# Top-k key selection with one candidate word and two small instructions per bit

## The chip, the cores and the metric

The kernel runs on one core of a Trainium2 chip. The metric is device time in microseconds (us) of one launch; lower is better. The engines are named as the profile names them: PE (matrix multiplication; PEld is its weight load), DVE (vector), ACT (scalar), POOL (GpSimd) and SP (its queue issues most DMAs).

## What is computed

The reference is one inference step of a two-layer decoder for a prompt of 1024 tokens and for 8 sequences of 8 new tokens each. Layer 0 mixes with RWKV-7, layer 1 with sparse attention, and each layer has a feed-forward part. The change lies in the sparse attention. There, an indexer gives every query a score for every key, and only the 256 keys with the highest scores are attended to:

```python
def select_keys(qi, wi, ki, pos_q, topk):
    L = ki.shape[1]
    logits = jnp.einsum('bthd,bsd->bths', qi.astype(F32), ki.astype(F32)) * IDX_DIM ** -0.5
    score = jnp.einsum('bths,bth->bts', jax.nn.relu(logits), wi.astype(F32))
    pos_k = jnp.arange(L)
    adm = pos_k[None, None, :] <= pos_q[None, :, None]
    _, idx = lax.top_k(jnp.where(adm, score, -jnp.inf), topk)
    valid = idx <= pos_q[None, :, None]
    return idx, valid
```

Ties go to the key with the lower index. The attention that follows is a softmax over the chosen keys.

## The kernel before

The 1024 prompt tokens are worked on in two groups. Group A (`GA`) is the 64 sample tokens and the first 512 prompt tokens, group B (`GB`) the last 512. Activations lie with features on the 128 partitions and tokens along the free axis. Every large product is three matmuls, high times high, low times high and high times low part (line 140, tiles `hi`/`lo` or `uh`/`ul` against `wh`/`wl`), into PSUM tiles `o` of 512 columns, of which there are four. DVE empties those of a residual product into `xr` (line 388). For group B one such matmul has 512 columns, for group A 320 or 256.

Layer 1's attention of a group goes by tiles of 128 queries. `att_post` normalises the projections and makes the indexer's scores in a tile `sc` (matmuls `ip`, DVE line 1149). `topk` turns scores into a bias of 0 or -1e30 in place. `att_tile` then makes attention scores (matmuls `sp`, lines 1168 and 1169; DVE line 1264 adds the bias), the softmax (ACT line 1268), transposes (`pt`) and sums over values (`po`). Queries before position 256 need no selection. Four calls of `topk` are left:

- group A, prompt tiles 3 and 4 together: scores of 384 and 512 keys for 128 queries each, beside the attention of tiles 1 and 2 and the sample's indexer (`sample_index`, matmuls `kip`, `il`, `iw`);
- the sample: 64 queries by 2056 keys, beside the attention of tiles 3 and 4; its bias goes through HBM into `att_sample2`, which starts with the transposes `qzp`;
- group B, tiles 0 and 1: 640 and 768 keys, beside `att_post` of tiles 2 and 3;
- group B, tiles 2 and 3: 896 and 1024 keys, beside the attention of tiles 0 and 1.

`topk` finds the 256th largest score of each query by its bits. Scores are taken as 32-bit words; `xm` is all ones for a query with fewer than 256 scores at or above zero, so that negative words can be searched by the same steps. From bit 30 down to bit 0, five things are done: a candidate word `cand` is the found word `m` with this bit set; `cf` is `cand` with the signs turned by `xm`; `count` counts the scores at or above `cf` read as a float, one instruction for each of the two score tiles (one for the sample), with the sum in `cnt`; `ok` says whether that is 256 or more; `m` takes `cand` where `ok` holds. For the upper 15 bits the counts read `ups`, 16-bit copies of the high halves of the scores, and for the lower 16 bits the scores themselves. Then equal scores are ranked (`teq`, `trk`) and the bias is written.

These routines are generators. `together` takes one step of each in turn, so a `topk` bit stands beside a step of an attention tile. A further generator, `side`, carries independent work: the rest of layer 0 and the projections of group B beside group A's attention, and layer 1's output projection and feed-forward of group A beside group B's attention. In group A's attention `RATES` gives it no steps inside `together` and it is written behind; in group B's it gets 0.2 or 0.3 of a step each round. A scheduler then sets the order of instructions on each engine when the program is built, and each engine works its own list in order. So what stands on PE between two attention products is settled before the run.

## Time and profile before

| | |
|---|---|
| median of 3 runs | 4378.32 us (4348.06 to 4389.85) |
| the profiled execution | 4376.47 us |
| its span, first to last instruction | 4374.7 us |
| mean granted TensorE clock | 0.912 |
| PE busy | 4008.7 us (92%) |
| DVE busy | 2647.1 us (61%) |
| ACT busy | 1681.9 us (38%) |
| POOL busy | 971.5 us (22%) |

A busy share is a mean over stages with different limits. Idle time of an engine costs something only in the stage where that engine's work ends last. A granted clock of 1.00 is 2.4 GHz; the other level is half of it, and a mean between the two tells how much of a stretch was at either.

### The profile page before, as it was taken

How to read it: one execution, taken by the hardware profiler on the slowest of the kernel's cores; microseconds unless marked ns; L12 is line 12 of the kernel's file. 1: busy time of each engine (PE TensorE's matmuls, PEld its weight loads, DVE VectorE, ACT ScalarE, POOL GpSimd, SP SyncE). 2: the span in 40 equal slices, each digit the busy share in tenths (PEclk: the TensorE clock that was granted, in tenths of full speed). 3: DMA queues.
4: the chain of work that ended last, by engine and by line, in shares of the span. 5: the costliest groups of instructions: out<-in, count | busy, mean ns of one | idle time of the engine just before them, and what ended most of it. 6: DMA issues, size and time to landing. Idle time of an engine off the chain costs nothing. (4 is left out here: it accounts for less than half of the span.)

```text
span 4374.7 us, 77889 instructions
## 1 busy us (share of the span) xinstructions
PE 4008.7 (92%) x31096; PEld 3205.7 (73%) x31096; DVE 2647.1 (61%) x6822; ACT 1681.9 (38%) x3169; POOL 971.5 (22%) x762
## 2 busy tenths in 40 slices
PE   7997899998999999989899888989778999999999
PEld 5796566666777799988655565778667667998887
DVE  5513766565677655552887964442899965555444
ACT  5533544443345333332444333332443333333333
POOL 1321222222333222211111122222110000222222
PEclk7797779998798999998899999998879999999999
DMA  6675222333221122234332145444211111322332
GB/s 224 211 237 183 66 65 78 99 89 95 59 56 51 45 80 82 78 114 140 102 84 67 53 153 193 141 128 151 69 50 41 40 39 34 116 87 90 96 96 87
DMA packets 506749, 433.94 MB, mean 99 GB/s; under 512 B 93777, under 2 KB 451777, under 8 KB 501202
## 3 DMA queue, kind: packets, MB, share of 16 engines
q1 hardware_dynamic: 500498, 391.20, 30.2%
q0 software_dynamic: 5888, 37.75, 2.5%
q8 instruction: 245, 4.01, 0.4%
q14 instruction: 118, 0.97, 0.1%
HBM read 360.48 MB, written 67.87 MB: 98 GB/s over the span
## 5 line engine op out<-in xcount | busy, mean ns | idle before, releaser
L126 POOL TENSOR_TENSOR wl<-w,wh 128x1024 fp32r<-128x1024 f32 (+1 forms) x258 | 615.8, 2391 | 2330.8 <-ACT wh L122 2076.9
L140 PE MATMUL o<-hi,wh 128*128 128x512 f32 (+4 forms) x2592 | 891.8, 347 | 27.3 <-ACT hi L144 23.6
L140 PE MATMUL o<-lo,wh 128*128 128x512 f32 (+4 forms) x2592 | 890.7, 345 | 18.4 <-DVE lo L145 14.1
L140 PE MATMUL o<-hi,wl 128*128 128x512 f32 (+4 forms) x2592 | 886.3, 343 | 2.5 <-DVE wl L126 2.3
L122 ACT CAST wh<-w 128x1024 fp32r<-128x1024 f32 (+3 forms) x388 | 396.4, 1035 | 985.8 <-PE o L140 816.0
L388 DVE SCALAR_TENSOR_TENSOR xr<-o,mods,xr 128x256 f32<-128x256 f32 (+1 forms) x816 | 463.3, 570 | 292.9 <-PE o L140 281.0
L140 PEld LDWEIGHTS o<-hi,wh 128*128 128x128 f32 (+1 forms) x2592 | 499.2, 194 | 86.6 <-ACT hi L144 28.8
L140 PE MATMUL o<-uh,wh 128*128 128x320 f32 (+2 forms) x1536 | 522.1, 340 | 41.5 <-DVE xr L388 33.0
L140 PEld LDWEIGHTS o<-lo,wh 128*128 128x128 f32 (+1 forms) x2592 | 500.2, 193 | 74.2 <-DVE lo L145 20.1
L140 PEld LDWEIGHTS o<-hi,wl 128*128 128x128 f32 (+1 forms) x2592 | 499.1, 193 | 50.8 <-issue 10.0
L140 PE MATMUL o<-uh,wl 128*128 128x320 f32 (+2 forms) x1536 | 515.3, 336 | 1.8 <-POOL wl L126 1.1
L140 PE MATMUL o<-ul,wh 128*128 128x320 f32 (+2 forms) x1536 | 516.7, 336 | 0.0
L140 PEld LDWEIGHTS o<-uh,wh 128*128 128x128 f32 x1536 | 294.3, 192 | 80.3 <-DVE xr L388 41.0
L140 PEld LDWEIGHTS o<-uh,wl 128*128 128x128 f32 x1536 | 294.2, 192 | 29.8 <-issue 5.7
L140 PEld LDWEIGHTS o<-ul,wh 128*128 128x128 f32 x1536 | 294.7, 192 | 28.0 <-issue 5.8
L126 DVE TENSOR_TENSOR wl<-w,wh 128x1024 fp32r<-128x1024 f32 (+2 forms) x130 | 183.6, 1412 | 216.5 <-ACT wh L122 212.1
L145 DVE TENSOR_TENSOR ul<-z,uh 128x512 fp32r<-128x512 f32 (+1 forms) x128 | 128.5, 1004 | 164.2 <-ACT uh L144 164.1
L1018 PE MATMUL o<-wl,hi 128*128 128x256 f32 (+2 forms) x648 | 188.1, 292 | 6.9 <-POOL wl L126 6.9
L1018 PE MATMUL o<-wh,hi 128*128 128x256 f32 (+2 forms) x648 | 187.1, 291 | 6.9 <-ACT hi L144 6.9
L1018 PE MATMUL o<-wh,lo 128*128 128x256 f32 (+2 forms) x648 | 183.9, 291 | 0.0
L1268 ACT ACTIVATE sm<-sm,st 128x128 f32<-128x128 f32 (+7 forms) x128 | 99.3, 776 | 139.4 <-DVE st L1267 83.8
L1018 PEld LDWEIGHTS o<-wl,hi 128*128 128x128 f32 (+1 forms) x648 | 126.8, 196 | 9.1 <-POOL wl L126 9.1
(411 smaller groups left out, 7063.1 us busy)
## 6 DMA issues: line engine op xcount, KB each, us to landing
w<-in_w_up SPq DMA_DIRECT2D x128, 512.0 KB
w<-in_w_down SPq DMA_DIRECT2D x128, 512.0 KB
wa<-in_w_ada SPq DMA_DIRECT2D x96, 512.0 KB
w<-in_rw_w_rkv SPq DMA_DIRECT2D x48, 512.0 KB
w<-in_att_w_in SPq DMA_DIRECT2D x32, 512.0 KB
RA<-pt SPq DMA_DIRECT2D x48, 288.0 KB
RB<-pt SPq DMA_DIRECT2D x48, 256.0 KB
in<-RA SPq DMA_DIRECT2D x32, 320.0 KB
```

The costliest lines, as they stand in the source:

```text
L122: nc.scalar.copy(h[:kp, :n], w[:kp, :n])
L126: eng.tensor_tensor(out=l[:kp, :n], in0=w[:kp, :n], in1=h[:kp, :n], op=ALU.subtract)
L140: nc.tensor.matmul(o[0:M, 0:c1 - c0], a, b[:, c0:c1], start=(i == 0 and q == 0), stop=(i == n - 1 and q == 2))
L145: (lo_eng or self.nc.vector).tensor_tensor(out=lo, in0=src, in1=hi, op=ALU.subtract)
L388: nc.vector.scalar_tensor_tensor(out=xm[:, p0:c1], in0=o[:, p0 - c0:c1 - c0], scalar=self.mods[l][:, j * 8 + m, 8:9], in1=xm[:, p0:c1], op ...
L1018: nc.tensor.matmul(o[0:n, 0:cw], a, w, start=(k == 0 and q == 0), stop=(k == 7 and q == 2))
L1268: nc.scalar.activation(out=sm[:, 0:L], in_=sm[:, 0:L], func=AF.Exp, scale=-1.0, bias=mn[:, 0:1], accum_out=sums)
```

## The change

`topk` keeps one word, `cf`, which is always the next candidate with its sign turned already. After the count, `no` is the current bit where the count was too small and 0 elsewhere. One instruction then makes the next candidate: `cf` xor `no` xor the next lower bit. So `cand`, `m`, `xm`, `ok` and the predicated copy are gone, and a bit has two small instructions beside its counts where it had four. The 16-bit copies are gone as well, with their step of the generator; all 31 counts read the 32-bit scores. The sample's call names one tile fewer in its placement.

```diff
-        m = T1("tm", [128, n], I32)[0:R]
-        cand = T1("tcand", [128, n], I32)[0:R]
         cf = T1("tcf", [128, n], I32)[0:R]
-        xm = T1("txm", [128, n], I32)[0:R]
-        ok = T1("tok", [128, n], I32)[0:R]
+        no = T1("tno", [128, n], I32)[0:R]
         junk = T1("tj", [128, Lm], BF16)[0:R]
 
-        ups = []
-        for i, s in enumerate(scs):
-            u = T1("tu%d" % i, [128, Lm], BF16)[0:R, 0:s.shape[1]]
-            nc.vector.tensor_copy(u, s.bitcast(BF16).rearrange("p (l b) -> p l b", b=2)[:, :, 1])
-            ups.append(u)
-        yield
-
-        def count(th, op, src):
-            for i, s in enumerate(src):
+        def count(th, op):
+            for i, s in enumerate(scs):
...
-        count(0.0, ALU.is_ge, scs)
-        nc.vector.tensor_scalar(out=xm, in0=cnt, scalar1=float(TOPK) - 0.5, scalar2=-1.0, op0=ALU.is_lt, op1=ALU.mult)
-        nc.vector.memset(m, 0)
+        count(0.0, ALU.is_ge)
+
+        nc.vector.tensor_scalar(out=no, in0=cnt, scalar1=float(TOPK) - 0.5, scalar2=-1.0, op0=ALU.is_lt, op1=ALU.mult)
+        nc.vector.tensor_scalar(out=cf, in0=no, scalar1=1 << 30, scalar2=None, op0=ALU.bitwise_xor)
+        th = cf.bitcast(F32)
         yield
         for b in range(30, -1, -1):
-            nc.vector.tensor_scalar(out=cand, in0=m, scalar1=1 << b, scalar2=None, op0=ALU.bitwise_or)
-            nc.vector.tensor_tensor(out=cf, in0=cand, in1=xm, op=ALU.bitwise_xor)
-            count(cf.bitcast(F32), ALU.is_ge, ups if b >= 16 else scs)
-            nc.vector.tensor_scalar(out=ok, in0=cnt, scalar1=float(TOPK) - 0.5, scalar2=None, op0=ALU.is_ge)
-            nc.vector.copy_predicated(m, ok, cand)
-            yield
-        nc.vector.tensor_tensor(out=cf, in0=m, in1=xm, op=ALU.bitwise_xor)
-        th = cf.bitcast(F32)
-        count(th, ALU.is_gt, scs)
+            count(th, ALU.is_ge)
+            nc.vector.tensor_scalar(out=no, in0=cnt, scalar1=float(TOPK) - 0.5, scalar2=float(1 << b), op0=ALU.is_lt, op1=ALU.mult)
+            if b:
+                nc.vector.scalar_tensor_tensor(out=cf, in0=no, scalar=1 << (b - 1), in1=cf, op0=ALU.bitwise_xor, op1=ALU.bitwise_xor)
+            else:
+                nc.vector.tensor_tensor(out=cf, in0=no, in1=cf, op=ALU.bitwise_xor)
+            yield
+        count(th, ALU.is_gt)
```

The built programs are the same on every engine up to the first selection of group A, and the same again on PE from 162 matmuls after the end of group B's attention on. In between the order has moved. In the changed kernel's rows, line 1187 is the count, 1197 makes `no`, 1199 the next `cf`, and the lines behind the search stand nine lower than before.

On DVE, two bits of group B's second selection beside the attention of tiles 0 and 1 (`sc` are the score tiles, `ql` a query's low part, `PT` a transposed probability tile). Before:

```order
L1204 TENSOR_SCALAR tcand<-tm 128x2
L1205 TENSOR_TENSOR tcf<-tcand,txm 128x2
L1197 TENSOR_SCALAR tj,cnt<-sc_35136,tcf 128x896
L1197 TENSOR_SCALAR tj,cnt<-sc_35137,tcf 128x1024
L1163 TENSOR_TENSOR ql<-qt,qh 64x512
L1207 TENSOR_SCALAR tok<-cnt 128x2
L1208 COPY_PREDICATED tm<-tok,tcand 128x2
L1204 TENSOR_SCALAR tcand<-tm 128x2
L1205 TENSOR_TENSOR tcf<-tcand,txm 128x2
```

Now:

```order
L1199 SCALAR_TENSOR_TENSOR tcf<-tno,tcf 128x2
L1187 TENSOR_SCALAR tj,cnt<-sc_34998,tcf 128x896
L1187 TENSOR_SCALAR tj,cnt<-sc_34999,tcf 128x1024
L1197 TENSOR_SCALAR tno<-cnt 128x2
L1199 SCALAR_TENSOR_TENSOR tcf<-tno,tcf 128x2
L1187 TENSOR_SCALAR tj,cnt<-sc_34998,tcf 128x896
L1278 COPY PT<-pt 128x256
L1187 TENSOR_SCALAR tj,cnt<-sc_34999,tcf 128x1024
```

Between two pairs of counts two small instructions stand now instead of four. Over the four selections 13 emptyings of line 388 in group B and 7 in group A have moved behind the selection beside which they stood.

On PE, from the last indexer product of group B (`ip`) to the first attention score of tile 0 (`sp`), which follows the first selection of group B. `uh`, `ul` are the feed-forward's inner activations of group A, side work. Before:

```order
L1168 MATMUL ip<-kS,qh 128x512
L1169 MATMUL ip<-kS,ql 128x512
L140 MATMUL o<-uh,wl 128x320
L140 MATMUL o<-uh,wh 128x256
...
L140 MATMUL o<-ul,wh 128x320
L140 MATMUL o<-uh,wl 128x320
L1168 MATMUL sp<-kS,qh 128x512
L1169 MATMUL sp<-kS,ql 128x512
```

Now:

```order
L1168 MATMUL ip<-kS,qh 128x512
L1169 MATMUL ip<-kS,ql 128x512
L140 MATMUL o<-uh,wh 128x320
L140 MATMUL o<-ul,wh 128x320
...
L140 MATMUL o<-ul,wh 128x256
L140 MATMUL o<-uh,wl 128x256
L1168 MATMUL sp<-kS,qh 128x512
L1168 MATMUL sp<-kS,qh 128x128
```

193 matmuls of line 140 stood between, 72 stand there now, while on DVE, behind the last line 1149, 17 pairs of counts have become 14; at the last score product of group B's attention the side work is 169 such matmuls behind where it was. They come behind that attention, before the output projection of group B.

On PE, from the last value product of group A's prompt tiles (`po`) to the first transposes of the sample's attention (`qzp`), which wait for nothing of the selection but stand in the order behind it. `hi`, `lo` are group B's activations, side work. Before:

```order
L1291 MATMUL po<-PT,V 64x128 x7
L1296 MATMUL po<-c_ident,st 64x128 x2
L140 MATMUL o<-hi,wh 128x512
L140 MATMUL o<-lo,wh 128x512
...
L140 MATMUL o<-hi,wh 128x512
L140 MATMUL o<-lo,wh 128x512
L1462 MATMUL qzp<-c_ident,qns 128x64 x8
```

Now:

```order
L1282 MATMUL po<-PT,V 64x128 x7
L1287 MATMUL po<-c_ident,st 64x128 x2
L140 MATMUL o<-hi,wl 128x512
L140 MATMUL o<-hi,wh 128x512
...
L140 MATMUL o<-uh,wh 128x512
L140 MATMUL o<-ul,wh 128x512
L1453 MATMUL qzp<-c_ident,qns 128x64 x8
```

302 matmuls of line 140 stood between, 261 stand there now. With 19 more that have gone from before the last `po`, the side work is 60 matmuls behind where it was at `qzp`, and has caught up by the end of group B's feed-forward of layer 0.

## Rows read from the trace of the kernel before

**Rows 1.** The page's first part: the span, then by engine the busy us (share of the span) and count of instructions.

```profile
span 4374.7 us, 77889 instructions
...
PE 4008.7 (92%) x31096; PEld 3205.7 (73%) x31096; DVE 2647.1 (61%) x6822; ACT 1681.9 (38%) x3169; POOL 971.5 (22%) x762
```

**Rows 2.** Busy time of each engine in stretches of the span (from and to in us, the length, then busy us of PE, PEld, DVE, ACT and POOL with counts of instructions in brackets; last the granted TensorE clock, the DMA share and GB/s). 2190 to 2321 is group A's first selection, 2368 to 2527 the sample's bits and 2527 to 2555 its ranks, 3100 to 3303 group B's first selection (from 3257 on it is behind the last `ip`), 3303 to 3532 its second. 3532 to 3705 is the attention of group B's tiles 2 and 3. The last two are stretches of feed-forward alone, of group A and of group B.

```profile
2190.00:2321.00 131.00, 122.46 (x574) 70.75 (x572) 116.41 (x422) 58.51 (x150) 22.55 (x18) 0.95 0.32 86
...
2368.00:2527.00 159.00, 135.46 (x679) 94.33 (x677) 149.67 (x312) 50.60 (x94) 19.22 (x9) 0.91 0.18 52
2527.00:2555.00 28.00, 22.04 (x82) 16.90 (x81) 27.39 (x43) 5.59 (x8) 6.20 (x2) 0.88 0.25 76
...
3100.00:3257.00 157.00, 123.99 (x621) 100.02 (x620) 141.38 (x374) 68.31 (x125) 17.85 (x8) 0.78 0.16 51
3257.00:3303.00 46.00, 36.20 (x234) 34.17 (x233) 44.89 (x136) 11.15 (x17) 7.37 (x3) 0.85 0.20 58
3303.00:3512.00 209.00, 187.61 (x1195) 138.98 (x1193) 193.31 (x604) 70.61 (x141) 14.33 (x6) 0.94 0.15 41
3512.00:3532.00 20.00, 11.84 (x40) 7.60 (x40) 19.91 (x57) 5.12 (x9) 0.00 (x0) 0.70 0.00 0
3532.00:3705.00 173.00, 172.94 (x1223) 128.93 (x1222) 93.20 (x286) 69.59 (x123) 11.91 (x5) 0.99 0.15 40
3850.00:3900.00 50.00, 49.35 (x369) 48.84 (x368) 25.05 (x65) 16.54 (x24) 12.09 (x5) 1.00 0.28 85
4050.00:4100.00 50.00, 50.00 (x218) 40.60 (x217) 22.03 (x25) 17.99 (x25) 15.06 (x6) 1.00 0.34 102
```

**Rows 3.** PE's waits from 2190 to 2555: who waited for whom, total us, times, longest.

```profile
PE o L140 <- DVE xr L388: 12.9, 3, 8.6
PE sp L1169 <- DVE tok L1207: 5.3, 3, 2.7
```

**Rows 4.** DVE's groups of instructions from 2180 to 3520, different shapes together: the four small instructions of a bit over all selections, and the 16-bit copies (count | busy us, mean ns | idle before).

```profile
L1207 DVE TENSOR_SCALAR tok<-cnt 128x2 int32<-128x2 f32 (+1 forms) x124 | 32.0, 258 | 1.4
L1204 DVE TENSOR_SCALAR tcand<-tm 128x2 int32<-128x2 int32 (+1 forms) x124 | 22.7, 184 | 2.3
L1205 DVE TENSOR_TENSOR tcf<-tcand,txm 128x2 int32<-128x2 int32 (+1 forms) x124 | 22.1, 178 | 2.5
L1208 DVE COPY_PREDICATED tm<-tok,tcand 128x2 int32<-128x2 int32 x93 | 20.3, 218 | 1.5
...
L1208 DVE COPY_PREDICATED_SCALAR tm<-tok,tcand 64x1 int32 x31 | 6.3, 204 | 0.6
...
L1190 DVE COPY tu<-sc 128x384 bf16<-128x384 bf16 (+5 forms) x6 | 5.2, 886 | 0.0
...
L1190 DVE COPY tu<-ssc 64x2056 bf16<-64x2056 bf16 x1 | 1.2, 1222 | 0.0
```

**Rows 5.** DVE in order of time, one bit of group A's first selection with nothing between (start us, duration us).

```profile
2302.45 0.15 DVE L1204 TENSOR_SCALAR tcand<-tm 128x2 int32<-128x2 int32 x1
2302.64 0.16 DVE L1205 TENSOR_TENSOR tcf<-tcand,txm 128x2 int32<-128x2 int32 x1
...
2304.28 0.17 DVE L1207 TENSOR_SCALAR tok<-cnt 128x2 int32<-128x2 f32 x1
2304.48 0.16 DVE L1208 COPY_PREDICATED tm<-tok,tcand 128x2 int32<-128x2 int32 x1
```

**Rows 6.** DVE in order of time, a small instruction of group B's first selection with other work behind it.

```profile
3158.78 0.15 DVE L1207 TENSOR_SCALAR tok<-cnt 128x2 int32<-128x2 f32 x1
3158.85 0.74 DVE L1149 SCALAR_TENSOR_TENSOR sc<-rl,pr,sc 128x512 f32<-128x512 f32 x1
```

**Rows 7.** DVE and POOL in order of time, one small instruction of the same selection.

```profile
3203.53 2.39 POOL L126 TENSOR_TENSOR wl<-w,wh 128x1024 fp32r<-128x1024 f32 x1 [7.87 <-ACT wh L122]
...
3203.79 2.16 DVE L1207 TENSOR_SCALAR tok<-cnt 128x2 int32<-128x2 f32 x1
```

**Rows 8.** DVE in order of time, an instruction of the form of the new line 1199 on floats, in a normalisation.

```profile
1914.80 0.17 DVE L169 SCALAR_TENSOR_TENSOR rsAb<-rsAa,ms 128x5 f32<-128x5 f32 x1
```

**Rows 9.** DVE's groups by shape, 2180 to 3520: the sample's counts on 32-bit scores (`ssc`) and on their 16-bit copy (`tu`); then, prompt and sample and all shapes together, all counts on copies.

```profile
L1197 DVE TENSOR_SCALAR_CACHE_REDUCE tj<-ssc,tcf 64x2056 bf16<-64x2056 f32 x17 | 39.9, 2344 | 0.5
L1197 DVE TENSOR_SCALAR_CACHE_REDUCE tj<-tu,tcf 64x2056 bf16<-64x2056 bf16 x15 | 35.1, 2342 | 0.3
...
L1197 DVE TENSOR_SCALAR_CACHE_REDUCE tj<-tu,tcf 128x384 bf16<-128x384 bf16 (+3 forms) x105 | 119.8, 1141 | 1.8
```

**Rows 10.** DVE's emptying of residual products by shape, 2180 to 3520 (512 columns: group B's, 256: group A's).

```profile
L388 DVE SCALAR_TENSOR_TENSOR xr<-o,mods,xr 128x512 f32<-128x512 f32 x128 | 94.9, 745 | 55.2 <-PE o L140 54.8
...
L388 DVE SCALAR_TENSOR_TENSOR xr<-o,mods,xr 128x256 f32<-128x256 f32 x85 | 40.8, 481 | 8.3 <-PE o L140 8.0
```

**Rows 11.** PE in order of time, at the sample's selection, where it waited for DVE's emptying.

```profile
2506.75 0.40 PE L140 MATMUL o<-uh,wl 128*128 128x512 f32 x1
2515.73 0.80 PE L140 MATMUL o<-uh,wh 128*128 128x512 f32 x1 [8.58 <-DVE xr L388]
...
2516.75 0.63 PE L140 MATMUL o<-uh,wl 128*128 128x512 f32 x1
2517.18 0.63 PE L140 MATMUL o<-uh,wh 128*128 128x512 f32 x1
```

More of the change, by code (lines that the diff above doesn't have):

```diff
@@ L1405, in att_mixed @@
                 tiles = [None] + [self.att_tile(g, i, p2, S[i], 512) for i in range(1, 5)]
-                smp = [self.sample_index(p3, ssc, gather, ki_rows, csm), self.topk(p3, [ssc], 64, {"tj": ("kis", 1), "tu0": ("rls", 1), "teq": ("kiraw", 2), "trk": ("kiraw", 2)},
+                smp = [self.sample_index(p3, ssc, gather, ki_rows, csm), self.topk(p3, [ssc], 64, {"tj": ("kis", 1), "teq": ("kiraw", 2), "trk": ("kiraw", 2)},
                                                                                                    lambda s: [s[:, a * 1024:a * 1024 + 1024].rearrange("r (b c) -> r c b", b=2)[:, c0:c0 + 256]
```

## The prediction

> **What bounds the kernel now.** I read first the page's busy times [rows 1]. PE is busy 92% of the span and DVE 61%, so the first guess is that work on DVE is free. That share is a mean, however, so next I cut the span at the four selections [rows 2]. There it is the other way round. In group B's first selection DVE is busy 186.3 of 203 us (141.38 and 44.89) and PE 160.2, at a granted clock of 0.78 to 0.85; in its second DVE has 213.2 of 229 us and PE 199.5. In the sample's bits and ranks DVE has 177.1 of 187 us and PE 157.5. Only group A's first selection is nearer to PE: 122.46 of 131 us, against 116.41 for DVE. In the stretch after the selections, from 3532 to 3705, PE has 172.94 of 173 us and DVE 93.2. So the kernel changes its bound: DVE sets the pace beside a selection, PE sets it elsewhere.
>
> PE's waits confirm it [rows 3]: two of those in group A's attention are for the emptying of a product on DVE (12.9 us) and for `tok`, a small instruction of the search (5.3 us). One of them is seen in order of time [rows 11]: PE stands for 8.58 us, and its next matmuls come 0.43 us apart (2516.75 to 2517.18) instead of some 0.23; that is 1.2 GHz instead of 2.4.
>
> PE's idle time is what there is to win: 8.5, 23.5 and 6 us in group A and the sample, 33, 9.8, 21.4 and 8.2 us in group B [rows 2], 110 us in all. PE's work itself is not changed, and the list that PE works through is fixed. So a shorter selection gains only as much as PE then idles less, and what the scheduler has moved out of the selection's time must be paid for behind it.
>
> **The change part by part.** *Two small instructions less per bit.* With nothing between, small instructions start 0.20 us apart [rows 5] (2304.28 to 2304.48), so two less give 0.40 us a bit, 31 bits 12.4 us, four selections 49.6 us. The groups agree: all small instructions together have 32.0 + 22.7 + 22.1 + 20.3 + 6.3 = 103.4 us [rows 4], half of it 51.7. I take 50. The lower bound: where other work follows at once, a small instruction holds DVE for 0.07 us only [rows 6] (3158.78 to 3158.85), which makes 124 x 2 x 0.07 = 17 us. I keep near the upper end because in these stretches the bits mostly follow each other. The new instruction of line 1199 is not in the trace on integers; the same form on floats takes 0.17 us [rows 8], as much as the `tcf` before it, so I count it at that. It could cost no less than `tcf`'s 0.16, and at twice that it would take 124 x 0.17 = 21 us of the 50 away, which the low end of the range covers.
>
> One of these small instructions took 2.16 us [rows 7], while POOL worked for 2.39 us on a split: DVE stood until POOL was done. Such waits are in the 51.7 and nearly not in the 49.6. The Trainium skill (SBUF — State Buffer, "Who interferes with whom") says that VectorE and GpSimd share a port pair by an exclusive lock, and that an instruction with two SBUF inputs or a plain `tensor_scalar` contends for it. By that the two instructions that stay can each take over a wait of the two that go, so the waits would not be halved; the sum by it would be 49.6 instead of 51.7. The trace agrees with the lock as far as the one row goes.
>
> *No 16-bit copies.* Their seven instructions have 5.2 + 1.2 = 6.4 us [rows 4], shared by the number of keys 2.3 us in group A and 4.1 in group B. Nothing replaces them if a count costs the same on either kind of word, and it does: 2344 ns on 32 bits and 2342 on 16 for the sample's 2056 keys [rows 9]. The Trainium skill (VectorE: DVE Perf Modes, "The perf-mode tier table (the rule you actually need)") speaks against the change here: a `tensor_scalar` on bf16 in SBUF runs at 4x and on fp32 at 2x. By this rule alone the copies would halve their counts, and the sum would turn to a loss; the trace disagrees for the form that also writes a sum, by the pair of 2344 and 2342 ns.
>
> *One round less.* `topk` has one step fewer, so two rounds of group B's attention carry 0.2 of a side step less each: 21.3 instead of 21.7 in all, still 21 whole steps. That costs nothing. The few instructions at a selection's head and end (the clearing of `m`, the last xor) are under 0.3 us each time and I leave them out.
>
> *What the order moves out.* In group A's part 7 emptyings of 745 ns [rows 10] leave the selections, 5 us of DVE, and in group B's 13 of 481 ns, 6 us. With them go side matmuls: 60 of 512 columns in group A's part and 169 of 320 or 256 in group B's. They are paid for later at PE's full pace, 50 us / 218 = 0.229 us each and 50 us / 369 = 0.135 us each [rows 2]: 13.7 and 22.9 us. The emptyings cost nothing there, since DVE is half idle in those stretches (93.2 of 173 us, 22.0 of 50).
>
> *The sum.* Group A and the sample: 25 + 2.3 + 5 = 32 us shorter on DVE, 13.7 us paid back, 18 left. But half of that is from the first selection, where PE has only 8.5 of 131 us to give, so I take two thirds, 12 us. Group B: 25 + 4.1 + 6 = 35 us shorter, 22.9 paid back, 12 left; PE idles 72 us there, so this is not capped. Together 24 us. The profiled execution took 4376.47 us, 1.8 us more than its span and 1.9 us less than the median of the runs shown. 4376.5 - 24 = 4352 us is the forecast; the ends of the sum are 0 (with the 17 us for the small instructions: 17 + 6.4 + 11 = 34 saved, 36.6 paid back) and 56 us (all of DVE's relief).
>
> **The rivals.** *All of the relief arrives.* The moved matmuls find places where PE now stands: in the sample's attention behind the selection, or beside group B's tiles. Then nothing is paid back and the time is 4376.5 - 56 = 4320 us. For it speaks PE's idle time of 110 us; against it that PE is full from 3532 on [rows 2], where group B's 169 matmuls go.
>
> *Nothing arrives.* The scheduler has moved as much PE work out as the selections get shorter: 36.6 us. If small instructions are mostly hidden among other work [rows 6], DVE saves 34 us, and the time stays at 4377 us. The place where this is nearest is the join before group B's first attention scores: 121 of the 193 side matmuls are gone there (16 us), while the 17 bits that stood behind the last `ip` in the order have become 14, and a bit is worth 0.40 us.
>
> *Slower: PE starves at the joins.* With 72 matmuls (10 us) between the last `ip` and the first `sp`, and some 14 bits of search beside them, PE stands for most of the time that was 46 us long, falls to 1.2 GHz, and starts the next tile slowly. The stall of [rows 11] shows the price: matmuls 0.43 us apart instead of 0.23, 3.6 us behind each wait if I take it to last for 18 matmuls. If that comes at all four selections (14 us) and DVE's saving is the low 23 us without the emptyings, against 36.6 us paid back, the time is 4376.5 + 14 + 13.6 = 4404 us. It decides when DVE saves less than PE has to make up. PE's idle time of 72 us in group B's selections speaks for it; against it, that the search still has 0.40 us less in every bit.
>
> *Slower: 32-bit counts cost more.* If the 15 counts on copies came to cost twice as much on the scores, their 119.8 us [rows 9] would come on top, 58 us would go, and the time would be near 4440 us. The pair of 2344 and 2342 ns is against it. This is what the tier table of the Trainium skill, named above, would make of the change.
>
> **How the numbers follow.** The forecast of 4352 us has a chance of 0.54, all of the relief 0.18, nothing 0.20, starving 0.07 and dear counts 0.01. The range must leave out no more than 2 in 10: from 4318, just below the full relief, to 4386, which takes in the case of no gain and the half per cent that single runs of this kernel differ by (4348 to 4390). It leaves out 0.08 for the two slow cases and as much again for misjudged sums. About 1%, or 44 us, is what a measurement of this kernel can tell from no change. Faster by more needs less than 4334.5 us: the full relief, and the better tail of the forecast, 0.23. Slower by more needs over 4422 us: the dear counts and a worse case of starving, 0.05. That leaves 0.72 within 1%.
>
> **What the changed profile would show.** The counts keep their durations to a few ns, with twice `no` and `cf` at 0.13 to 0.20 us between them; DVE's busy time falls by 50 to 60 us. A bit of group A's first selection alone takes some 1.85 us instead of 2.25. The sample's bits end about 25 us sooner than at 2527, and group B's second selection about 50 us sooner than at 3532, reckoned from the start. PE's stretch after it is full and some 20 us longer. Up to 2190 us nothing moves. The forecast is wrong if PE's idle time in the selections does not fall (then nothing arrives), if PE's clock there drops under 0.78 (starving), or if the matmuls that moved stand in what are now PE's gaps (full relief). A line 1199 of 0.3 us or more would take a fifth or more of the gain.

## Result and the profile after

The changed kernel takes 4335.24 us (median of 12 runs, 4327.12 to 4357.13), the kernel before 4378.3 us in the runs beside it. The ratio is 0.9909 with a 95% interval of 0.9889 to 0.9929, so some 40 us are gone (31 to 49) where 24 were forecast. Run once more beside three of the experiments, it gave 0.9919 (0.9879 to 0.996).

The page after, its span and busy times:

```profile
span 4346.6 us, 77619 instructions
PE 4005.2 (92%) x31096; PEld 3205.6 (74%) x31096; DVE 2601.4 (60%) x6563; ACT 1679.1 (39%) x3169; POOL 972.6 (22%) x762
```

Against [rows 1] DVE has 45.7 us less to do, and PE's count is the same. The next rows are DVE's groups from 2180 to 3520 (count | busy us, mean ns | idle before), different shapes together: the new small instructions, and the sample's counts, now all on 32-bit words.

```profile
L1197 DVE TENSOR_SCALAR tno<-cnt 128x2 int32<-128x2 f32 (+1 forms) x124 | 29.7, 240 | 1.0
L1199 DVE SCALAR_TENSOR_TENSOR tcf<-tno,tcf 128x2 int32<-128x2 int32 (+1 forms) x120 | 26.5, 221 | 1.7
L1201 DVE TENSOR_TENSOR tcf<-tno,tcf 128x2 int32<-128x2 int32 (+1 forms) x4 | 0.6, 154 | 0.1
...
L1187 DVE TENSOR_SCALAR_CACHE_REDUCE tj<-ssc,tcf 64x2056 bf16<-64x2056 f32 x32 | 74.9, 2340 | 0.5
```

The small instructions have 29.7 + 26.5 + 0.6 = 56.8 us, where [rows 4] had 103.4. A count costs 2340 ns, as much as either kind in [rows 9]. One bit of group A's first selection alone, DVE in order of time (start, duration; READ_ACCUMULATOR is the end of a count):

```profile
2256.37 0.75 DVE L1187 TENSOR_SCALAR_CACHE_REDUCE tj<-sc,tcf 128x512 bf16<-128x512 f32 x1
2257.04 0.08 DVE L1187 DVE_READ_ACCUMULATOR tj<-sc,tcf 128x1 f32 x1
2257.16 0.17 DVE L1197 TENSOR_SCALAR tno<-cnt 128x2 int32<-128x2 f32 x1
2257.36 0.16 DVE L1199 SCALAR_TENSOR_TENSOR tcf<-tno,tcf 128x2 int32<-128x2 int32 x1
2257.56 0.61 DVE L1187 TENSOR_SCALAR_CACHE_REDUCE tj<-sc,tcf 128x384 bf16<-128x384 f32 x1
2258.10 0.08 DVE L1187 DVE_READ_ACCUMULATOR tj<-sc,tcf 128x1 f32 x1
2258.22 0.75 DVE L1187 TENSOR_SCALAR_CACHE_REDUCE tj<-sc,tcf 128x512 bf16<-128x512 f32 x1
```

From one count to the same count of the next bit it is 1.85 us (2256.37 to 2258.22), and the small instructions start 0.20 us apart, as in [rows 5].

To see where the time went, both traces are cut at the same events instead of the same times. The columns are those of [rows 2]. The stretches are, in this order: the sample's upper 15 bits; its lower 16; from its last count to the transposes `qzp`; the upper 15 bits of group B's first selection; the upper 15 and then the lower 16 of its second; and everything from the first count of group A's first selection to the last matmul. Before:

```profile
2369.30:2450.09 80.79, 70.00 (x377) 45.65 (x375) 75.99 (x171) 28.57 (x60) 5.82 (x3) 0.94 0.17 46
2450.09:2527.30 77.21, 64.46 (x294) 47.89 (x295) 72.71 (x143) 21.63 (x34) 13.71 (x7) 0.89 0.20 58
2527.30:2570.77 43.47, 32.76 (x128) 25.40 (x126) 31.93 (x46) 10.40 (x14) 11.91 (x7) 0.92 0.40 114
3127.29:3233.95 106.66, 77.71 (x341) 58.81 (x341) 96.64 (x264) 54.81 (x102) 7.17 (x3) 0.73 0.13 43
3324.15:3410.40 86.25, 77.41 (x488) 57.16 (x485) 79.95 (x249) 25.46 (x55) 4.79 (x2) 0.92 0.12 33
3410.40:3512.00 101.60, 95.94 (x640) 71.04 (x638) 92.94 (x301) 38.15 (x73) 7.14 (x3) 0.98 0.18 46
2191.86:4368.93 2177.07, 1997.27 (x12086) 1576.53 (x12084) 1389.71 (x3301) 782.46 (x1326) 410.44 (x238) 0.94 0.30 90
```

After:

```profile
2377.44:2442.82 65.38, 60.31 (x342) 40.37 (x340) 64.66 (x125) 26.81 (x52) 7.16 (x3) 1.00 0.21 58
2442.82:2512.96 70.14, 59.83 (x284) 45.30 (x283) 68.44 (x109) 20.65 (x33) 14.65 (x6) 0.95 0.21 65
2512.96:2547.04 34.08, 25.50 (x99) 20.14 (x99) 31.54 (x48) 7.60 (x10) 7.72 (x5) 0.85 0.27 71
3107.96:3196.21 88.25, 59.26 (x280) 45.69 (x278) 82.80 (x218) 43.84 (x84) 10.63 (x5) 0.71 0.15 47
3287.56:3367.54 79.98, 76.74 (x505) 57.10 (x504) 74.51 (x217) 28.98 (x60) 7.08 (x3) 0.97 0.18 47
3367.54:3463.77 96.23, 91.46 (x588) 67.64 (x586) 84.46 (x258) 34.98 (x68) 4.74 (x2) 0.93 0.11 30
2205.72:4340.49 2134.77, 1980.63 (x12089) 1568.00 (x12087) 1344.11 (x3044) 781.35 (x1327) 412.30 (x238) 0.95 0.30 92
```

Two things are read from the last rows. From the first count on the kernel takes 2134.77 us instead of 2177.07, 42.3 less. PE's idle time in it (the length less PE's busy time) fell from 179.8 to 154.1 us, which is 25.7 of that. The other 16.6 are PE's busy time: the same matmuls at a granted clock that was more often 2.4 GHz. To three digits the mean clock of these rows is 0.943 before and 0.949 after; what is missing to 1.000 makes 124 and 109 us, a difference of 15.

Ahead of the first count nothing has changed in the order on any engine but two copies of under 2 us, and yet this count began at 2191.86 us before and at 2205.72 after; in the other profiled executions of this study at anything from 2183 to 2212. So single executions scatter by up to 29 us in code that is the same. Behind the first count they do so less: two executions of one kernel agreed there within 1.4 us (changed kernel 2134.8 and 2136.1; the kernel of the first experiment 2143.6 and 2144.7). But the kernel before and two kernels of the experiments that are changed in group B alone (e4 and e10) have the same order on PE, DVE, ACT and POOL up to one emptying behind the sample's last output, and it starts 593.4, 600.0 and 588.4 us behind their first counts (at 2191.86, 2196.88 and 2187.71 us):

```profile
2785.26 0.75 DVE L388 SCALAR_TENSOR_TENSOR xr<-o,mods,xr 128x512 f32<-128x512 f32 x1 [0.63 <-PE o L140]
2796.89 0.75 DVE L388 SCALAR_TENSOR_TENSOR xr<-o,mods,xr 128x512 f32<-128x512 f32 x1 [0.63 <-PE o L140]
2776.12 0.75 DVE L388 SCALAR_TENSOR_TENSOR xr<-o,mods,xr 128x512 f32<-128x512 f32 x1 [0.64 <-PE o L140]
```

I therefore take 12 us as what a comparison of two executions from the first count can tell. Behind group B's first count it is 3 us: kernels with the same order there took 1279.2 and 1282.2 us (before and e3), and 1266.1, 1268.1 and 1268.2 us (the changed kernel twice and e4).

### The profile page after: what moved, and what is told of

Its sections match the earlier page's. It is cut to its first block, busy times and chain, and to the rows that moved or that the text cites. A ratio compares the mean times of both kernels' runs of the same rounds, so it can differ in the third digit from the quotient of the medians.

```text
span 4346.6 us, 77619 instructions
## 1 busy us (share of the span) xinstructions
PE 4005.2 (92%) x31096; PEld 3205.6 (74%) x31096; DVE 2601.4 (60%) x6563; ACT 1679.1 (39%) x3169; POOL 972.6 (22%) x762
## 5 line engine op out<-in xcount | busy, mean ns | idle before, releaser
L140 PE MATMUL o<-hi,wh 128*128 128x512 f32 (+4 forms) x2592 | 886.7, 345 | 27.4 <-ACT hi L144 22.7
L140 PE MATMUL o<-uh,wh 128*128 128x320 f32 (+2 forms) x1536 | 522.1, 340 | 39.4 <-DVE xr L388 29.7
L1187 DVE TENSOR_SCALAR_CACHE_REDUCE tj<-sc,tcf 128x384 bf16<-128x384 f32 (+2 forms) x192 | 180.4, 940 | 2.4
L1259 ACT ACTIVATE sm<-sm,st 128x128 f32<-128x128 f32 (+7 forms) x128 | 99.3, 776 | 154.1 <-DVE st L1258 106.4
```

Of the source, the lines that this page charges most:

```text
L140: nc.tensor.matmul(o[0:M, 0:c1 - c0], a, b[:, c0:c1], start=(i == 0 and q == 0), stop=(i == n - 1 and q == 2))
L1187: nc.vector.tensor_scalar(out=junk[:, 0:L], in0=s, scalar1=th if isinstance(th, float) else th[:, i:i + 1], scalar2=None, op0=op, op1=ALU. ...
L1259: nc.scalar.activation(out=sm[:, 0:L], in_=sm[:, 0:L], func=AF.Exp, scale=-1.0, bias=mn[:, 0:1], accum_out=sums)
```

## Experiments

Theory 1 is the prediction's: a shorter selection is worth DVE's time, less the PE work that the new order leaves to make up. Theory 2 holds the new order for a chance gain. Theory 3, formed after the first results: the scheduler takes counts on 16-bit words for shorter than they are, so it lays too little other work beside the upper bits, and PE stands. Theory 3 has a part that no run shows, what the scheduler takes a count for; its consequences can be tested. The table has for each kernel the ratio over whole runs, and from its profiled execution the times from group A's first count: to the first count of group B (all of group A's attention and what is made up behind it) and to the end, with PE's idle and busy time in the latter.

| kernel | ratio [95%] | to B's first count, us | to the end, us | PE idle | PE busy |
|---|---|---|---|---|---|
| before | 1 | 897.9 | 2177.1 | 179.8 | 1997.3 |
| e1, no copies | 0.9881 [0.9845, 0.9918] | 878.4 | 2143.6 | 169.1 | 1974.5 |
| e1 again | 0.9890 [0.9848, 0.9931] | 879.4 | 2144.7 | 163.4 | 1981.3 |
| e2, two small only | 0.9961 [0.9938, 0.9984] | 881.7 | 2164.3 | 161.5 | 2002.8 |
| e3, new in group A | 0.9904 [0.9871, 0.9938] | 871.3 | 2153.5 | 164.3 | 1989.2 |
| e4, new in group B | 0.9953 [0.9930, 0.9976] | 902.2 | 2170.4 | 173.5 | 1996.9 |
| e5, two unread | 0.9937 [0.9912, 0.9962] | 874.2 | 2146.0 | 160.7 | 1985.3 |
| e6, more side work | 0.9887 [0.9852, 0.9921] | 869.6 | 2140.5 | 159.7 | 1980.8 |
| e7, all 16-bit | 0.9995 [0.9978, 1.0012] | 898.2 | 2183.3 | 185.1 | 1998.3 |
| e8, copies unread | 0.9951 [0.9928, 0.9974] | 881.3 | 2147.2 | 172.6 | 1974.6 |
| e9, more side work twice | 0.9879 [0.9824, 0.9935] | 865.6 | 2137.0 | 155.5 | 1981.5 |
| e10, before with more side work | 1.0010 [0.9980, 1.0040] | 893.2 | 2179.0 | 180.2 | 1998.8 |
| after | 0.9909 [0.9889, 0.9929] | 868.6 | 2134.8 | 154.1 | 1980.6 |
| after again (e11) | 0.9919 [0.9879, 0.9960] | 868.0 | 2136.1 | 153.8 | 1982.3 |

**No copies, four small instructions (e1, and once more).** The kernel before; the copies are left out, and every count reads the scores.

```diff
...
-            u = T1("tu%d" % i, [128, Lm], BF16)[0:R, 0:s.shape[1]]
-            nc.vector.tensor_copy(u, s.bitcast(BF16).rearrange("p (l b) -> p l b", b=2)[:, :, 1])
...
-            count(cf.bitcast(F32), ALU.is_ge, ups if b >= 16 else scs)
+            count(cf.bitcast(F32), ALU.is_ge, scs)
```

> The kernel before with one part of the change alone: the 16-bit copies are gone and all 31 counts read the 32-bit scores; the four small instructions of a bit stay. Theory 1 (DVE's time beside a selection comes back, less the PE work that goes behind it): only the copies' 6.4 us leave DVE, so 2 to 6 us less, ratio 0.999 (0.997 to 1.001). Theory 2 (the order that the scheduler happens to lay decides, not DVE's time): the order moves here too, so the ratio may lie anywhere between 0.992 and 1.008. Counts of equal duration on both kinds of word, 2340 to 2346 ns for the sample, in either theory.

> The kernel before without the 16-bit copies, a second time: the first gave 0.9881 (0.9845 to 0.9918) where 6.4 us were expected. Theory 3: 108 more side matmuls stand before the last value product of group B than in the kernel before (11348 and 11240) and 30 more before the sample's last output (8062 and 8032), 15 and 7 us of PE, with the copies' 6.4 us near 28 us: ratio 0.9935 (0.990 to 0.996). Theory 1: 0.999.

Measured: 0.9881 and 0.989, and 33 and 32 us less from the first count on. Theory 1 falls as to this part: copies of 6.4 us of DVE cannot give 33. The first ratio is also below theory 2's 0.992 and the second below theory 3's 0.990. In whole runs the ratios mean 52 and 48 us of 4378, as much as the whole change or more; why the traces give less is open.

**Two small instructions, copies and 16-bit counts kept (e2).** The changed kernel with the copies put back and the upper 15 counts on them; the diff shows the count.

```diff
-            count(th, ALU.is_ge)
+            count(th, ALU.is_ge, ups if b >= 16 else scs)
```

> The changed kernel with the 16-bit copies put back and the upper 15 counts on them: only the two small instructions per bit are gone. Theory 1: 50 of 56 us of DVE's relief, so about nine tenths of the 40 us of the change, ratio 0.992 (0.990 to 0.995). Theory 2: not tied to that, anywhere between 0.988 and 1.004.

Measured: 0.9961 (17 us, 7 to 27), outside theory 1's 0.990 to 0.995, and 12.8 us less from the first count on: 16.2 less in group A's part and 3 more in group B's. PE's idle time fell by 18.3 us, its busy time rose by 5.5. The upper 15 bits of group B's second selection, and the whole from the first count:

```profile
3308.67:3388.16 79.49, 69.66 (x355) 49.52 (x354) 66.89 (x185) 22.10 (x47) 4.70 (x2) 0.74 0.13 34
2211.81:4376.06 2164.25, 2002.80 (x12086) 1580.20 (x12084) 1348.66 (x3049) 782.99 (x1326) 413.27 (x238) 0.94 0.30 91
```

Its granted clock there is 0.74, where the kernel before has 0.92 and the changed one 0.97: in bits that are shorter, with 355 matmuls beside them instead of 488, PE stands for 10 of 79 us and more of its matmuls run at 1.2 GHz. Behind group B's first count PE's busy time rose by 11 us (1202.2 against 1191.2) while its idle time fell by 7.6. That is the starving of the prediction's third rival, in this stretch of this kernel.

**New routine in one group only (e3 in A, e4 in B).**

```diff
-                self.together(RATES["post2B"], post[2:4], [self.topk(tk, S[0:2])])
+                self.together(RATES["post2B"], post[2:4], [self.topk_old(tk, S[0:2])])
...
-            self.together(RATES["tile0B"], tiles[0:2], [self.topk(tk, S[2:4])])
+            self.together(RATES["tile0B"], tiles[0:2], [self.topk_old(tk, S[2:4])])
```

The diff is e3's, against the changed kernel, with `topk_old` the routine before; e4 has the two calls of group A on the old routine.

> The new search in the two selections of group A's attention (prompt tiles 3 and 4, and the sample), the old one in group B's. Theory 1 by the traces: from the first count to the norm before group B's projections the changed kernel was 27 us shorter, so ratio 0.994 (0.992 to 0.996). My forecast's sum, which capped this part: 12 us, 0.997. Theory 2: a number that does not add up with the run for group B to the 40 us of the change.

> The new search in the two selections of group B's attention, the old one in group A's. Theory 1, and the forecast's sum: 12 to 13 us less, ratio 0.997 (0.995 to 0.999), and together with the run for group A 40 us. Theory 2: no such sum.

Measured: 0.9904 and 0.9953; from the first count on 23.6 and 6.7 us less. Group A's part accounts for the larger half of the gain (26.6 us of it by group B's first count); the forecast had 12 and 12, and e3's ratio is better than theory 1's 0.992 to 0.996. The two totals make 30 of the whole change's 42 us, but that shows no lack: e4's part in group A, where it is unchanged, came 4.3 us longer than before, and e3's in group B 3.0, both within the scatter. Where each has the new routine they gained 26.6 and 11.0 us, together 37.6. By whole runs they make 42 and 21 us, more than the whole. The traces speak for a sum and against theory 2 here, and the whole runs decide nothing.

**Two unread small instructions in each bit (e5).** The changed kernel; their results go nowhere.

```diff
+            nc.vector.tensor_scalar(out=d1, in0=no, scalar1=1 << b, scalar2=None, op0=ALU.bitwise_or)
+            nc.vector.tensor_tensor(out=d2, in0=d1, in1=no, op=ALU.bitwise_xor)
```

> The changed kernel with two more small instructions per bit that nobody reads (an or of the bit into `no`, an exclusive or of the result), so that DVE has four small instructions per bit again while the chain from count to count keeps its two. The scheduler lays PE's side work as in the changed kernel: 11068 matmuls stand before the last value product of group B's attention, 11078 in the changed kernel, 11240 in the kernel before. Theory 1 (the two small instructions gain by DVE's time): the 50 us on DVE come back with the order of the changed kernel, so most of the 40 us is lost, ratio 0.998 to 1.006 against the kernel before. Theory 3 (the gain comes from what the removal of the copies does to the order, the small instructions are worth little): near the changed kernel, 0.989 to 0.995.

Measured: 0.9937, as theory 3 had it; 11.2 us more from the first count on than the changed kernel. The premise failed: the pair was to put 50 us back on DVE, and its busy time behind the first count rose by only 18 (1362.18 against 1344.11), 0.07 us for each of 248. Nothing waits for their results, so the next instruction starts at once, as in [rows 6].

```profile
2207.25:4353.26 2146.01, 1985.30 (x12089) 1570.09 (x12087) 1362.18 (x3292) 783.04 (x1327) 412.90 (x238) 0.95 0.31 92
```

So 18 us of DVE's time seem to cost 11 by the traces and 12 by the ratios, but neither is clear of the scatter. It does not show the price of an instruction in the chain from count to count either, and so it does not test theory 1.

**Every bit on 16-bit words (e7).** The kernel before; the lower 16 bits are searched on the copies too, so the low halves of the scores are left out.

```diff
-            count(cf.bitcast(F32), ALU.is_ge, ups if b >= 16 else scs)
+            count(cf.bitcast(F32), ALU.is_ge, ups)
```

> The kernel before with all 31 counts of the search on the 16-bit copies, so the lower 16 bits of the threshold are left unresolved: part of the computation is left out, and the time is that of the same instructions on the other operand. A count takes the same time on either kind of word, so DVE's work is unchanged. Theory 3 (the scheduler takes a count on 16-bit words for shorter than it is, and lays too little beside it): 72 fewer side matmuls stand before the sample's first transposes and 25 fewer before the last value product of group B, so it is slower than the kernel before by 5 to 25 us, ratio 1.001 to 1.006. Theory 1: no difference, 0.998 to 1.002.

Measured: 0.9995, as theory 1 had it; 6.3 us more from the first count on, of which group A's part has 0.3. Theory 3 missed: by whole runs nothing is lost, and the 6 us of group B's part are little beside e1's gain. What 16-bit counts cost there was paid already by the upper bits, or the gain of e1 has another cause; no run tells which.

**Copies made but unread (e8).** The kernel before; only what the counts read is changed.

```diff
-            count(cf.bitcast(F32), ALU.is_ge, ups if b >= 16 else scs)
+            count(cf.bitcast(F32), ALU.is_ge, scs)
```

> The kernel before with its 16-bit copies still made, but read by nobody: all 31 counts take the 32-bit scores. Only what the counts read is changed. In the built program the side work stands 162 matmuls ahead of the kernel before at group B's last value product (108 in the kernel without copies), and 17 ahead at group A's. Theory 3 (the scheduler lays more side work beside counts on 32-bit words): the gain of the kernel without copies stays here nearly whole, since the copies' own instructions are 6.4 us; ratio 0.988 to 0.992. Rival (the gain of the kernel without copies comes from the copies' own work and its place at a selection's head): the gain is gone, 0.996 to 1.000.

Measured: 0.9951, between the two expectations, but from the first count on 29.9 us less, of which 16.6 by group B's first count: nearly e1's 33 and 19.5. The same stretches as above, up to the fifth, and the whole:

```profile
2364.13:2451.10 86.97, 82.67 (x488) 55.55 (x487) 82.46 (x188) 36.90 (x76) 9.48 (x4) 1.00 0.23 61
2451.10:2525.39 74.29, 59.25 (x257) 46.12 (x255) 72.20 (x128) 18.95 (x26) 14.80 (x6) 0.91 0.21 61
2525.39:2560.31 34.92, 24.24 (x95) 19.41 (x95) 31.66 (x47) 7.61 (x10) 9.84 (x6) 0.85 0.30 83
3111.13:3209.05 97.92, 72.94 (x339) 54.26 (x339) 96.54 (x265) 55.00 (x104) 9.40 (x3) 0.76 0.15 47
3297.80:3401.08 103.28, 98.68 (x620) 71.22 (x616) 90.77 (x301) 36.61 (x75) 4.78 (x2) 0.95 0.16 39
2192.33:4339.50 2147.17, 1974.56 (x12086) 1563.89 (x12084) 1391.50 (x3301) 780.60 (x1326) 414.19 (x238) 0.95 0.30 92
```

By whole runs e8 gained 21 us (11 to 32), clear of no change, so reading other words, with nothing saved on DVE, brings time. How much of e1's gain that is stays unsure: nearly all of it by the traces, less than half by whole runs (21 of 52 and 48). With e2 it makes up the change by either measure: 29.9 + 12.8 = 42.7 us of 42.3 by the traces, 21 + 17 = 38 of 40 by whole runs.

By the traces the copies' own time is the small part. The rest comes with the order: DVE's busy time is that of before (1391.50 against 1389.71), and neither the counts' duration nor their number has changed. Of the 29.9 us 22.7 are PE's busy time, at a mean clock of 0.95 instead of 0.94, and 7.2 its idle time. In the sample's upper bits PE does 488 matmuls in 86.97 us instead of 377 in 80.79, idles 4.3 us instead of 10.8, and runs at 1.00 instead of 0.94; DVE has 17 instructions more there. In the lower bits fewer matmuls stand than before (257 instead of 294). Group B's first upper bits take 9 us less with 339 matmuls instead of 341, and DVE idles only 1.4 us there, where it idled 10.

**Side work laid in by hand (e10, e6 and e9).** e10 is the kernel before with one number changed; e6 is the changed kernel with `post2B=0.3`, e9 with `post2B=0.3, tile0B=0.3`.

```diff
-RATES = dict(wkvA=0, wkvB=0.1, postA=0, tile1A=0, tile3A=0, seq=0, post0B=0.3, post2B=0.2, tile0B=0.2, tile2B=0.2)
+RATES = dict(wkvA=0, wkvB=0.1, postA=0, tile1A=0, tile3A=0, seq=0, post0B=0.3, post2B=0.2, tile0B=0.4, tile2B=0.2)
```

> The kernel before, key selection untouched, with one number changed: the share of side work beside the attention of group B's tiles 0 and 1 goes from 0.2 to 0.4 of a step each round. In the built program 162 side matmuls more stand before group B's last value product, 14 emptyings more lie beside its second selection, and nothing else moves. Theory 3 says that the order alone is worth something: 162 matmuls by 0.135 us are 22 us at most, less what PE cannot fit in; ratio 0.995 to 0.997. Theory 1 (DVE sets the pace beside the selection, so work laid there lengthens it by as much): 0.999 to 1.002.

> The changed kernel with 0.3 instead of 0.2 side steps per round beside group B's first selection. 137 more side matmuls then stand before the last value product of group B's attention (11215 instead of 11078), 18 us of PE at full pace. If PE idles in that selection and DVE can empty them (theory 3): 5 to 18 us faster than the changed kernel, ratio 0.986 to 0.990 against the kernel before. If DVE is the bound there (theory 1), they only lengthen the selection: 0.990 to 0.994.

> The changed kernel with the share of side work at 0.3 beside both of group B's selections; the built program has 324 side matmuls more before group B's last value product than the changed kernel, the same number as the kernel before with copies unread. If the selections of the changed kernel still leave PE idle, 324 by 0.135 us are 44 us at most, and half of that gives 0.986; if DVE sets the pace there as fully as it did, the emptyings that come with them (some 24 of 0.48 us) lengthen it by 12 us and the kernel stays where it was, 0.990 to 0.993.

Measured: 1.001, as theory 1 had it, 0.9887 and 0.9879. In e10 group B's second selection, upper and lower bits, and the whole:

```profile
3314.98:3401.74 86.76, 77.45 (x488) 57.31 (x485) 80.12 (x249) 25.45 (x55) 4.79 (x2) 0.92 0.12 33
3401.74:3518.47 116.73, 111.36 (x753) 87.55 (x752) 105.59 (x330) 41.66 (x78) 9.95 (x5) 0.97 0.17 45
2187.71:4366.67 2178.96, 1998.81 (x12086) 1578.31 (x12084) 1396.02 (x3301) 782.25 (x1326) 409.76 (x238) 0.94 0.30 90
```

The 162 matmuls (113 of them beside the lower bits) lengthen the lower bits from 101.60 to 116.73 us and the stretch from group B's first count to the last value product of its attention by 27 us; behind it 20.3 us come back. They cost there at least what they give back, 0.125 us each. PE was busy for 95.94 of 101.60 us there, and DVE for 92.94: there was no gap. e8 has the same 3595 matmuls between group B's first count and the last value product of its attention. That stretch in e8 and in e10:

```profile
3073.59:3708.11 634.52, 564.85 (x3595) 439.53 (x3596) 517.53 (x1504) 236.57 (x435) 61.59 (x26) 0.92 0.17 46
3080.86:3734.09 653.23, 579.32 (x3595) 450.66 (x3596) 523.72 (x1504) 238.05 (x435) 59.23 (x26) 0.90 0.16 45
```

e8 takes 18.7 us less for the same number of matmuls and of instructions on DVE. So, in group B, it is not the amount of side work beside a selection that e8 gains by, but its place. e6 and e9 agree by their traces: 137 and 324 matmuls more, and 2140.5 and 2137.0 us from the first count on, against 2134.8 and 2136.1 for the changed kernel. e6's ratio lies in the range of theory 3 and e9's between the two cases, but their intervals take in the changed kernel's ratio too. Neither they nor e1 can be told from the changed kernel by their ratios; none beats it for certain.

**The changed kernel again (e11).**

> The changed kernel once more, unaltered, on the same chip as the three runs beside it, to compare them with it directly: 0.989 to 0.993.

Measured: 0.9919, 2136.1 us from the first count on.

## Why the prediction was right or wrong

The time lies in the range, on the side forecast and within 1% of before, as the forecast had it with a chance of 0.72; but 40 us came where the sum had 24, and the sum was made of partly wrong terms. That the time stayed in the range is in part luck: the range was wide enough for the two rivals beside it, and the term that grew was not thought of.

*Two small instructions less.* The price on DVE was right: 103.4 us became 56.8, 46.6 less where I took 50, with `no` and `cf` at 0.17 and 0.16 us undisturbed. The lower bound by [rows 6] was not needed. DVE's busy time fell by 45.7 us, under the forecast 50 to 60. What it brings alone is 12.8 us by e2's trace (17 by its whole runs). Beside e1 it brings 9 us by the traces (2143.6 to 2134.8), within the scatter, and nothing by whole runs (0.9881 and 0.989 with four instructions, 0.9909 and 0.9919 with two), so what it adds there is not shown. By the traces all of it lies in group A's part (16 and 10 us) and nothing in group B's, where I had 12 left over. In e2 PE's clock took it back.

*The waits for POOL.* Of the 103.4 us about 24 were over the undisturbed 0.15 to 0.17 us an instruction, and of the 56.8 about 16 are (56.8 less 124 of 0.17 and 124 of 0.16). Two thirds of the waits stayed for half of the instructions. In the traces 18 of the small instructions take over 0.25 us before and 12 after, and each of them ends within 0.05 us of the end of an instruction on POOL, as in [rows 7]. So the instructions that stay took over some waits of those that went. The Trainium skill (SBUF — State Buffer, "Who interferes with whom") names an exclusive lock on a port pair that VectorE and GpSimd share; the trace agrees.

*No 16-bit copies.* This is the step that failed. "Nothing replaces them if a count costs the same" was true of DVE's time: 2340 ns after, against 2342 and 2344 in [rows 9], and 2344 in e8. It was not true of the order. That term of 6.4 us measured 33 us in e1's trace, of which 30 remain in e8's with the copies still made; by whole runs it is 52 and 48 us, of which 21 (11 to 32) remain. In group B, where the traces agree within 3 us, e1 and e8 with their four small instructions gain 14.0 and 13.3 us behind the first count, as much as the whole change (13.0). I had read the moved matmuls off the order of the whole change and taken them as an effect of shorter bits. By the traces most of the gain, by whole runs half of it, comes from where other instructions stand among the counts once these read 32-bit words.

*What the order moves out.* Group B's bill was right: [rows 2] gave 22.9 us, and from the second selection's last count on the kernel takes 19.8 us more (876.7 against 856.9). That this work was free where it had stood was never claimed, and e10 shows that it was not. Group A's bill was 13.7 us forecast for 60 matmuls; 8.3 were measured (37.6 us ahead at `qzp`, 29.3 at group B's first count), but for the 42 that are made up by then (3625 matmuls there instead of 3583). That is no contradiction.

*The cap of two thirds in group A.* I let 12 us through where 29 came, since PE had only 8.5 us to give in the first selection. For that selection the cap was right: it ends 19.9 us sooner, with 64 matmuls fewer beside it, but the sample's first count comes only 5.7 us sooner (171.7 us behind the first count instead of 177.4). What I had too small is the sample: 22.5 us in its bits and 9.4 behind its last count, less the 8.3 paid back, where the other half of my 18 us was 9. Behind the last count DVE's tail, in which the old order waited, is shorter. PE's waits in that stretch (total us, times, longest), before:

```profile
PE qzp L1462 <- DMA qns<-PA: 4.7, 1, 4.7
PE o L140 <- DVE xr L388: 3.6, 1, 3.6
PE o L140 <- DVE wl L126: 2.3, 1, 2.3
```

and after:

```profile
PE o L140 <- DVE xr L388: 10.1, 1, 10.1
PE qzp L1453 <- issue: 1.6, 1, 1.6
PE o L140 <- DVE wl L126: 0.4, 1, 0.4
```

`qzp` no longer waits for the transfer of `qns`, and DVE not for a split's `wh`, for which it stood 5.6 us before. The stretch is 34.08 us instead of 43.47, with 99 matmuls instead of 128. This step was nowhere in my sum. e1, e5, e7 and e8 have it too (34 to 37 us), e10 with the old order does not (43.3). What it is worth by itself is not shown: in e1 and e8 `qzp` still waits 3 us for `qns`, and e7, 13.9 us ahead at `qzp`, has lost all of it by group B's first count. A stall like that of [rows 11] is still there, of 10.1 us, now behind the last count.

*Signs.* The bit alone came at 1.85 us as said. The sample's counts ended 28.2 us sooner (25 said) and group B's second selection 62 (50 said), from the first count; reckoned from the start, as I had it, 14 and 48, since the first count came 13.9 us later. The clock fell under 0.78 in places, to 0.71 in group B's first upper bits (0.73 before) and to 0.60 in the 19 us behind that selection (0.82 before), without making the kernel slower. By that sign the forecast would have been wrong; the sign was badly chosen. "Up to 2190 us nothing moves" held for the order; the time there scattered by 14 us.

*The rivals.* "All of the relief" is about as near as the forecast, by amount (56 us and 24, 40 came), but not by its reason: the moved work was paid back. "Nothing" and "slower" did not come. Dear 32-bit counts are ruled out by 2340 ns. Starving, which I feared at the join before group B's first attention scores, did not come there. I had misread the join: [rows 2] has it from 3257 us to the end of the selection, but the last `ip` ended at 3235.84, and the first `sp` began at 3278.39, 27 us before the selection's last count ended. It does not wait for the selection. From the last `ip` to the first `sp`, before and after:

```profile
3235.84:3278.39 42.55, 31.11 (x198) 29.92 (x198) 41.11 (x119) 9.34 (x14) 7.33 (x3) 0.82 0.23 62
3217.45:3230.10 12.65, 10.73 (x77) 10.09 (x77) 12.63 (x42) 1.75 (x4) 0.00 (x0) 1.00 0.20 42
```

With fewer matmuls the join got shorter, and PE neither stood for most of it nor lost its clock. Something like starving came in e2, in group B's second selection.

**What stays open.** Why the order is better with 32-bit counts. Theory 3 fits e8 in the sample and in group B's second selection: more work beside the upper bits, though the counts take the same time on the chip. It does not fit group B's first, where 339 matmuls stand beside them instead of 341 and 9 us are gone all the same. e7, its opposite, cost at most 6 us, and e10 shows that more work beside a selection is worth nothing where both engines are full. What the scheduler takes a 16-bit count for was argued, not shown. Open too is why whole runs give e1 15 to 20 us more than its traces, and e8 9 less: each trace is one execution. Theory 2 cannot be told from theory 3 by one program of each kind; both say that e8's gain belongs to this order and not to the copies.

## What to carry to other kernels

Where a scheduler sets the order, an operand's type can be worth more through the order that it leads to than through the instruction's own time: rebuild with that one change alone, and keep the old work in, before giving it a price. Before more side work is laid beside a stage, look at both engines there: in the lower bits that e10 filled up, with PE busy 94% and DVE 91% before, it cost at least what it gave back. In e6 it did so too beside a selection where PE stands for 29 of 88 us but DVE is busy 94%: 17.7 us more up to the end of group B's attention, 12.9 back behind it. And compare executions from the first instruction that differs, not from the start: here that cut the scatter from 29 us to 12, and to 3 behind group B's first count. How large it is must be read from kernels whose order is the same, and whole runs can still say something else.

## What the runs showed of the hardware

The count, a `tensor_scalar` that also writes a sum, takes the same time on 16-bit and 32-bit words in these kernels: 2342 ns on 31 counts of 16-bit words in e7 and 2344 ns on 32 of 32-bit words in e8, for 2056 elements. A small instruction whose result nobody awaits takes 0.07 us of DVE (18 us for 248 in e5), one in the chain 0.20 us from start to start. A small instruction that met POOL's work ended with it: all 18 before and all 12 after that took over 0.25 us. I had not expected that of the 42 us behind the first count 16.6 would be PE's busy time, and 22.7 of e8's 29.9, by the clock: where PE waits less, the matmuls behind the waits are faster too.
